# 1/rms rows by a store and a broadcast load instead of TensorE spreads, block differences on VectorE, another order of the first x loads

## The chip, the cores and the metric

The kernel runs on one core of a Trainium2 chip. The metric is the time of one execution in device microseconds (us). Runs of the kernel before took 1004.34, 1004.38 and 1006.59 us, with a median of 1004.38.

## The reference

One layer of a decoder for 2048 prompt tokens and 8 decode tokens, model width 1024, all in float32:

```python
h = rmsnorm(x, norm_g)                    # x * rsqrt(mean(x*x) + eps) * g
p = h @ w_in                              # 1024 -> 8 groups of 512 columns
rq, rk, rv, rg, hq, hf, hi, hgate = split(p, 8)
o_ret = decay_recurrence(rotary(rq), rotary(rk), rv, fixed decay per head)   # 4 heads of 128
o_hg  = decay_recurrence(silu(hq), (1 - lb) * sigmoid(-hf), hi, learned decay)   # 4 heads of 128
o_ret = head_rmsnorm(o_ret, ret_g) * silu(rg);  o_hg = head_rmsnorm(o_hg, hg_g) * silu(hgate)
y = rmsnorm(x + concat(o_ret, o_hg) @ w_out, final_norm_g)
```

It returns y for both kinds of token and the final states. What the change touches is the factor 1/rms = rsqrt(mean(x*x) + eps) of the first rmsnorm, one number for each token.

## The kernel before

**Products.** Each float32 operand is split into a high and a low part, and a product is three matmuls (high by high, high by low, low by high). Most of the large products are products of 2×2 blocks done with seven products of sums and differences of blocks: weights A11, S1, S2, S4, A12, S3, A22 against x blocks B11, T1, T2, B22, B21, T3, T4 (in the value phase the roles are exchanged). One such product for a 512-column tile is twelve matmuls of 128x512, called a position here; seven positions are a unit. PSUM tiles of a unit are called aV, eV, bV in the value phase (aG, aR, aH later).

**Order of the work.** Code puts its steps on a heap by position (`at(pos, f)`, and `after(d, f)` for d positions later); most positions are numbers of the table AT. They are taken off in order of position, and each engine then runs its own instructions in that order: TensorE, VectorE, ScalarE, POOL (GpSimd) and SP, which issues most of the loads. An engine that waits holds up everything queued behind it.

**Phases.** First comes a warm-up of TensorE: 13 matmuls of 128x128 and AT['wu'] tiny ones (L203). Then the value phase makes the columns rv and hi for eight groups of 256 tokens, in the order 4, 5, 6, 7, 0, 1, 2, 3 (V_ORDER; `i` is the place in it, so that group 6 is i=2). The groups i=0 and 1 are done by plain products (L465, PSUM tile pv), those from i=2 on in units of seven positions (L872). Then come 24 units for the other six column groups, the recurrences between them, and eight output units.

**1/rms in the value phase.** For each group, `stats_load` (L324) loads x rows with tokens on the partitions (tiles xn), ScalarE squares and sums them (L332), and POOL makes 1/rms of it (`root`, L336 and L229) into rs_all, tokens on the partitions. But x is multiplied in its transposed form (tiles xr, loaded by `tok_load`, L312, 512 KB for each of two halves), with tokens along the row: there 1/rms must lie along the row and be the same on all partitions. For that `spread_dg` (L356) lets VectorE multiply an identity by 1/rms, twice for a group, and `spread` (L363) multiplies these diagonals by a matrix of ones on TensorE; PSUM tile prs then holds the row on all partitions. `tok_norm` (L372) multiplies x by g and by prs on VectorE. `tok_sums` (L393 to L399) forms the block sums S1 to S4, `s_split` (L271, L272) splits them into s2S, s3S and so on (the number is i).

**The same elsewhere.** For the decode tokens `decode_dg` and `decode_spread` (L583) do this with 8 columns. For the second swap of x blocks, `x1_dg` and `x1_spread` make two rows of 512 tokens by a diagonal, four matmuls (`blk_spread`, L701, PSUM tile prb), a copy on ScalarE and a store by POOL into rb_dram, which `x1_rb` loads eight times (L1345).

**Block differences.** For i=6 and 7, `blocks_sums` (L424 to L439) forms T1 to T4 of x in two halves (n), four subtractions each (tiles bT, bs), and POOL stores them (L430). `less` (L434) puts the halves (6, 0) and (7, 1) on VectorE, (6, 1) and (7, 0) on POOL.

**Buffers.** Short-lived tiles come from a round of buffers (`t_get`, `t_done`): the one that was given back longest ago is used next, so that a tile more or fewer changes which buffer every later tile gets. Weights of a unit are loaded 5.6 positions ahead of it, and first used on VectorE 2.4 positions ahead of it.

The value outputs are added up in tiles vo (L716, from PSUM) and stored into v_dram by SP (L461).

Of the kernel before, what the change touches and what calls it, by code (L numbers as in the profile page):

```python
# [19 lines left out]
P = 128  # L20
# [28 lines left out]
def spooled(u):  # L49
# [79 lines left out]
 'wu': 17,  # L129
# [14 lines left out]
 'dhs': (-5.0, -2.2, -2.2, -1.5)}  # L144
# [5 lines left out]
def step_kernel(ctx, tc, a, out):  # L150
# [22 lines left out]
    vd_dram = dr.tile([2, NB, GW], F32, tag="vd_dram", name="vd_dram")  # L173
    v_dram = [
# [151 lines left out]
    def stats_sum(i, ahead=False):  # L326
        p = V_ORDER[i]
        ms = sm.tile([P, 4], F32, tag="ms", name=f"ms{p}")
        for j in range(2):
            for h in range(2):  # L330
                r = xn.pop((2 * p + j, h))
                act.activation(r, r, AF.Square, accum_out=ms[:, 2 * h + j : 2 * h + j + 1])  # L332
                t_done(r)

        def root():
            pool.tensor_tensor(ms[:, 0:2], ms[:, 0:2], ms[:, 2:4], op=ALU.add)  # L336
            rsqrt_mean(rs_all[:, 2 * p : 2 * p + 2], ms[:, 0:2], D, EPS)

        if ahead:
            root()  # L340
        else:
            after(0.5, root)
# [7 lines left out]
    dgs = {}  # L350

    def spread_dg(i):
        dgs[i] = []
        for c in (2 * V_ORDER[i], 2 * V_ORDER[i] + 1):
            dg = vq.tile([P, P], F32, tag="dg", name=f"dg{c}", bufs=2)
            dve.tensor_scalar(dg, ident, rs_all[:, c : c + 1], None, op0=ALU.mult)  # L356
            dgs[i].append(dg)

    def spread(i):
        p = V_ORDER[i]  # L360
        pt = ps_tr.tile([P, 2, P], F32, tag="tr", name=f"prs{p}")
        for j, dg in enumerate(dgs[i]):
            pe.matmul(pt[:, j], ones, dg, start=True, stop=True)  # L363
        spread_to[i] = pt.rearrange("p a b -> p (a b)")
# [59 lines left out]
    def blocks_sums(i, n):  # L424
# [8 lines left out]
        def less(o, x, y):  # L433
            (dve if (i, n) in ((6, 0), (7, 1)) else pool).tensor_tensor(o, x, y, op=ALU.subtract)  # L434
# [35 lines left out]
    def tok_load0(i, k0, cuts=1):  # L470
        r = x0r[i, k0] = t_get([P, 2, 256], f"x0r{i}{k0}")
        for n in range(0, 2, 2 // cuts):
            kk = slice(n, n + 2 // cuts)
            sp.dma_start(r[:, kk], a["x_t"][V_ORDER[i], :, k0 + kk.start : k0 + kk.stop])
# [101 lines left out]
    dgd = vq.tile([NB, NB], F32, tag="dgd", name="dgd")  # L576

    def decode_dg():
        dve.tensor_scalar(dgd, ident[:NB, :NB], rsd[:, 1:2], None, op0=ALU.mult)

    def decode_spread():
        pt = ps_tr.tile([P, NB], F32, tag="tr", name="prsd")
        pe.matmul(pt, ones[:NB, :], dgd, start=True, stop=True)  # L583
        rb = vq.tile([P, NB], F32, tag="rbd", name="rbd")
        act.activation(rb, pt, AF.Copy)
        dve.tensor_tensor(
            xz[:, : 32 * KT].rearrange("p (k b) -> p k b", b=32)[:, :, :NB], xs,
            rb.unsqueeze(1).to_broadcast([P, KT, NB]), op=ALU.mult,
# [12 lines left out]
    tok_load0(0, 0, 2)  # L601
    wv_load(0, 2)
    act.activation(lb[:, 0:1], zero, AF.Sigmoid)
    tok_load0(0, 4)
    wv_load(4, 2)
    for k in (0, 4):
# [43 lines left out]
    with tc.manual_schedule(engines=ORDERED):  # L650
# [15 lines left out]
        spread_dg(2)  # L666
        ps = plain_next(1, 1, lambda: spread(2))
# [30 lines left out]
    def blk_spread(blk, dg, dst):  # L698
        pt = ps_tr.tile([P, 4, P], F32, tag="tr", name=f"prb{blk}")
        for j in range(4):  # L700
            pe.matmul(pt[:, j], ones, dg[:, j], start=True, stop=True)  # L701
        act.activation(dst, pt.rearrange("p a b -> p (a b)"), AF.Copy)

# [89 lines left out]
    def prep_events(u):  # L793
# [6 lines left out]
        for n, name in enumerate(("A11", "S3", "A22", "A12")):  # L800
            at(U + {0: -7.6, 1: -8.6}.get(u, w["load"] if u % 3 or u >= 12 else w["load0"]) + 0.5 * n, lambda name=name: w_load(u, name))
        if u < 12:
# [6 lines left out]
            at(U + d["sel"], lambda: dec_sel(u))  # L809
        at(U + w["S1"], lambda: w_s1(u))  # L810
# [501 lines left out]
    rb_dram = dr.tile([2, P, GW], F32, tag="rb_dram", name="rb_dram")  # L1312

    def x1_dg(n):
        dg = xd["dg", n] = t_get([P, 4, P], f"dgx{n}")
        dve.tensor_tensor(
            dg, ident.unsqueeze(1).to_broadcast([P, 4, P]),
            rs_all[:, 8 + 4 * TB[n] : 12 + 4 * TB[n]].unsqueeze(2).to_broadcast([P, 4, P]), op=ALU.mult,
        )

    def x1_spread(n):
        dg, rb = xd.pop(("dg", n)), t_get([P, GW], f"rbx{n}")
        blk_spread(2 + n, dg, rb)
        t_done(dg)

        def store():
            pool.dma_start(rb_dram[n], rb)
            t_done(rb)

        after(0.5, store)  # L1330

# [11 lines left out]
    def x1_rb(n, k):  # L1343
        xd["rb"] = t_get([P, GW], f"rb{n}{k}")
        sp.dma_start(xd["rb"], rb_dram[n])  # L1345
# [353 lines left out]
    V_POS = dict(norm=(2.1, 3.1), half=(4.7, 7.6), sums=(4.1, 6.0), s=(5.2, 6.7, 8.6, 9.6), blocks=(5.0, 5.8))  # L1699
    for i in range(2, 7):  # L1700
        U = 7 * (i - 8)
        at(U + 0.3, lambda i=i: spread_dg(i + 1))
        at(U + 1.6, lambda i=i: spread(i + 1))
# [8 lines left out]
        if i < 6:  # L1712
            at(U + 2.7, lambda i=i: tok_load(i + 2))
            at(U + 0.8, lambda i=i: stats_load(i + 2))
            at(U + 3.2, lambda i=i: stats_sum(i + 2))
# [6 lines left out]
    at(-42 + 5.2, decode_norm)  # L1722
# [12 lines left out]
    at(-21 + 3.6, decode_dg)  # L1735
    at(-21 + 5.6, decode_spread)
# [16 lines left out]
    def rec_events(u):  # L1753
# [7 lines left out]
        for n, pos in AT["ret" if u % 3 else "hgrn"].items():  # L1761
# [8 lines left out]
    for n in range(2):  # L1770
        at(9.2 + n, lambda n=n: x1_dg(n))
        at(10.6 + n, lambda n=n: x1_spread(n))
# [144 lines left out]
```

## Time and profile before

| | |
|---|---|
| median of three runs | 1004.38 us |
| the profiled execution | 1006.96 us |
| its span in the trace | 1005.2 us |
| TensorE busy | 987.3 us, 98% |
| VectorE busy | 783.6 us, 78% |
| ScalarE busy | 574.6 us, 57% |
| POOL busy | 256.2 us, 25% |
| DMA | 244.56 MB, mean 243 GB/s |

Times in the views are microseconds from the start of the span. PE is TensorE's matmul side and PEld its weight loads; DVE is VectorE, ACT ScalarE, SPq the queue of SyncE. A row of a timeline has start, duration, engine, line of the kernel, operation, output and inputs, shape and the count of like instructions in a row; `[0.16 <-DVE dg L356]` at its end is idle time of the engine ahead of the row and what released it. Float32 matmuls that aren't split, such as the spreads, are recorded as two passes each. Matmuls overlap, so the time that one takes of TensorE is read from the distance of the starts and not from the duration.

### The profile page before, as it was taken

How to read it: one execution, taken by the hardware profiler on the slowest of the kernel's cores; microseconds unless marked ns; L12 is line 12 of the kernel's file. 1: busy time of each engine (PE TensorE's matmuls, PEld its weight loads, DVE VectorE, ACT ScalarE, POOL GpSimd, SP SyncE). 2: the span in 40 equal slices, each digit the busy share in tenths (PEclk: the TensorE clock that was granted, in tenths of full speed). 3: DMA queues.
4: the chain of work that ended last, by engine and by line, in shares of the span. 5: the costliest groups of instructions: out<-in, count | busy, mean ns of one | idle time of the engine just before them, and what ended most of it. 6: DMA issues, size and time to landing. Idle time of an engine off the chain costs nothing.

```text
span 1005.2 us, 22979 instructions
## 1 busy us (share of the span) xinstructions
PE 987.3 (98%) x8824; PEld 822.0 (82%) x8824; DVE 783.6 (78%) x1361; ACT 574.6 (57%) x1348; POOL 256.2 (25%) x404
## 2 busy tenths in 40 slices
PE   9999999999999999999999999999999999999997
PEld 8788877888888888888788788888888878877885
DVE  6797696879869978887898766877866799767774
ACT  7754523847655664765885555456467577524332
POOL 0211271112332433232012222222222602313121
PEclk9999999999999999999999999999999999999999
DMA  9746659838958878785985993993996396674522
GB/s 332 242 150 238 222 189 357 313 114 298 305 171 306 304 239 287 279 253 184 348 261 175 303 321 119 304 335 109 309 370 218 111 406 228 238 263 155 206 88 83
DMA packets 121340, 244.56 MB, mean 243 GB/s; under 512 B 12128, under 2 KB 52448, under 8 KB 118544
## 3 DMA queue, kind: packets, MB, share of 16 engines
q1 hardware_dynamic: 97968, 164.68, 48.9%
q0 software_dynamic: 22976, 78.17, 21.0%
q8 instruction: 69, 1.13, 0.5%
q14 instruction: 39, 0.32, 0.1%
q10 hardware_dynamic: 288, 0.27, 0.1%
HBM read 155.97 MB, written 90.24 MB: 245 GB/s over the span
## 4 chain that ended last, share of the span: by engine, by line
PE 84%; DVE 7%; ACT 4%; issue 2%; DMA 1%; POOL 1%; POOLq 0%; SPq 0%; DVEq 0%; ACTq 0%
PE aH L872 9%; PE aG L872 8%; PE aO L872 7%; PE aR L872 7%; PE aV L872 5%; PE eG L872 4%; PE eH L872 4%; PE pv L465 4%; PE eO L872 4%; PE eR L872 3%; PE eV L872 2%; PE bH L872 2%; PE bG L872 2%; PE bO L872 2%; PE bR L872 2%
## 5 line engine op out<-in xcount | busy, mean ns | idle before, releaser
L1639 ACT ACTIVATE yj<-xro 128x512 f32<-128x512 f32 x24 | 15.2, 632 | 66.9 <-DVE xro L716 33.2
L1202 ACT ACTIVATE qh<-kh 128x1024 f32<-128x1024 f32 x24 | 25.5, 1061 | 47.3 <-DVE kh L1188 47.3
L1188 DVE TENSOR_TENSOR kh<-kh,fph 128x512 f32<-128x512 f32 x48 | 32.9, 686 | 11.4 <-PE plh L1223 10.5
L949 ACT ACTIVATE sg<-g 128x512 f32<-128x512 f32 x26 | 16.4, 631 | 36.3 <-DVE g L716 35.8
L1082 ACT ACTIVATE obh<-poh 128x128 f32<-128x128 f32 x64 | 16.9, 287 | 32.5 <-PE poh L1078 32.5
L1191 DVE TENSOR_TENSOR qth<-qth,fph 128x512 f32<-128x512 f32 x48 | 32.9, 685 | 0.0
L1082 ACT ACTIVATE obr<-por 128x128 f32<-128x128 f32 x64 | 16.8, 276 | 27.3 <-PE por L1078 27.3
L716 DVE TENSOR_TENSOR xro<-aO,xro 128x512 f32<-128x512 f32 x33 | 22.5, 685 | 8.1 <-PE aO L872 7.8
L1106 POOL DMA_DIRECT2D o_dram<-gth x16 | 12.4, 773 | 62.6 <-DVE gth L1103 23.4
L1090 ACT ACTIVATE obh<-poh,orsh 128x128 f32<-128x128 f32 x64 | 18.2, 366 | 16.5 <-POOL orsh L229 16.4
L336 POOL TENSOR_TENSOR ms<-ms 128x2 f32<-128x2 f32 x8 | 3.0, 370 | 95.4 <-ACT xn L332 95.4
L956 POOL DMA_DIRECT2D g_dram<-g x31 | 16.9, 548 | 39.0 <-DVE g L952 33.9
L1090 ACT ACTIVATE obr<-por,orsr 128x128 f32<-128x128 f32 x64 | 18.2, 368 | 14.6 <-POOL orsr L229 14.6
L228 POOL TENSOR_SCALAR orsh<-omsh 128x4 f32<-128x4 f32 x16 | 4.9, 308 | 84.1 <-ACT obh L1082 83.8
L902 ACT ACTIVATE vo<-aV 128x512 f32<-128x512 f32 x12 | 7.1, 592 | 32.4 <-PE aV L872 32.1
L1069 DVE SCALAR_TENSOR_TENSOR sth<-sth,fph,puh 128x128 f32<-128x128 f32 x48 | 16.7, 347 | 11.0 <-PE poh L1078 8.5
L1106 POOL DMA_DIRECT2D o_dram<-gtr x16 | 12.5, 782 | 46.3 <-DVE g L716 14.0
L1076 PE MATMUL poh<-vh,A 128*128 128x128 f32 x128 | 24.0, 274 | 0.0
L1076 PE MATMUL por<-vr,A 128*128 128x128 f32 x128 | 24.0, 274 | 0.0
L228 POOL TENSOR_SCALAR orsr<-omsr,pk 128x4 f32<-128x4 f32 x16 | 7.6, 474 | 57.5 <-ACT obr L1082 57.5
L1653 DVE SCALAR_TENSOR_TENSOR xro<-xro,yms,fg 128x1024 f32<-128x1024 f32 (+1 forms) x16 | 19.9, 1245 | 3.0 <-POOL yms L1650 3.0
L1078 PE MATMUL poh<-sth,qth 128*128 128x128 f32 x112 | 21.7, 275 | 0.0
(1712 smaller groups left out, 3760.0 us busy)
## 6 DMA issues: line engine op xcount, KB each, us to landing
xn<-in_x_prompt SPq DMA_DIRECT2D x32, 256.0 KB, 4.7
v_dram<-vo SPq DMA_DIRECT2D x32, 256.0 KB, 3.4
xro<-in_x_prompt SPq DMA_DIRECT2D x16, 512.0 KB, 5.8
g_dram<-g POOLq DMA_DIRECT2D x31, 256.0 KB, 5.6
out_y_prompt<-xro POOLq DMA_DIRECT2D x15, 512.0 KB, 3.4
xr<-in_x_t SPq DMA_DIRECT2D x12, 512.0 KB, 5.7
vh<-v_dram SPq DMA_DIRECT2D x16, 256.0 KB, 8.0
gth<-g_dram SPq DMA_DIRECT2D x16, 256.0 KB, 6.8
```

The source lines that it names most:

```text
L465: pe.matmul(ps, xx, ww, start=(first and n == 0), stop=(last and n == 2))
L716: dve.tensor_tensor(o, x, y, op=ALU.add)
L872: pe.matmul(ps, w[i], x[j], start=(first and k == 0 and m == 0), stop=(k == 3 and m == 2), skip_group_check=True,)
L1076: pe.matmul(po[:, j], s_ctx["A"][:, c], box["v"][g][:, j], start=True, stop=src is None)
L1078: pe.matmul(po[:, j], qcol(c), src, start=False, stop=True)
L1082: act.activation(ob[:, j], po[:, j], AF.Square, accum_out=ms[:, j : j + 1])
L1090: act.activation(ob[:, j], po[:, j], AF.Copy, scale=rs[:, j : j + 1])
L1106: after(AT["gate"]["tr"], lambda: pool.dma_start(o_dram[c0 : c0 + 4, ty, :, h].rearrange("c p t -> p c t"), gt.rearrange("p (c t) -> p c t ...
L1188: dve.tensor_tensor(kv[:, :, 0, :], kv[:, :, 0, :], two[:, :, 1:2].to_broadcast([P, nb, b]), op=ALU.mult)
L1191: dve.tensor_tensor(qv[:, :, 1, :], qv[:, :, 1, :], two[:, :, 0:1].to_broadcast([P, nb, b]), op=ALU.mult)
L1202: act.activation(kept_k, k, AF.Copy)
L1653: dve.scalar_tensor_tensor(x[:, cc], x[:, cc], ms[:, 0:1], fg[:, cc], op0=ALU.mult, op1=ALU.mult)
```

## The change

There are four parts.

1. 1/rms goes through DRAM. `root` also stores the 256 numbers of its group into rs_dram (POOL's queue), and `spread` is now a load of them by SP, broadcast to all partitions, into an SBUF tile rsb, which `tok_norm` reads. The diagonals and the matmuls are gone. The decode row goes the same way (store at position −35 + 3.6, load at −35 + 5.6, the multiply stays at −21 + 5.6), and `x1_rb` loads from rs_dram, so that `x1_dg`, `x1_spread`, `blk_spread` and rb_dram are gone.
2. All subtractions of `blocks_sums` are on VectorE.
3. The first x rows and weights are loaded in another order: the first k-slice of x's first half, the first weights, the first slice of the second half, the next weights, and then the two other slices.
4. AT['wu'] is 38 instead of 17.

The diff also names a few positions in the table ('vp', 'vl', 'hd', 'retL', 'hgrnL', 'w24'); they hold the numbers that stood there or in the code before, so these lines are left out here.

```diff
- 'wu': 17,
+ 'wu': 38,
...
+    rs_dram = dr.tile([T // P, P], F32, tag="rs_dram", name="rs_dram")
...
             rsqrt_mean(rs_all[:, 2 * p : 2 * p + 2], ms[:, 0:2], D, EPS)
+            pool.dma_start(rs_dram[2 * p : 2 * p + 2].rearrange("c p -> p c"), rs_all[:, 2 * p : 2 * p + 2])
...
-    def spread_dg(i):
-        dgs[i] = []
-        for c in (2 * V_ORDER[i], 2 * V_ORDER[i] + 1):
-            dg = vq.tile([P, P], F32, tag="dg", name=f"dg{c}", bufs=2)
-            dve.tensor_scalar(dg, ident, rs_all[:, c : c + 1], None, op0=ALU.mult)
-            dgs[i].append(dg)
-
     def spread(i):
         p = V_ORDER[i]
-        pt = ps_tr.tile([P, 2, P], F32, tag="tr", name=f"prs{p}")
-        for j, dg in enumerate(dgs[i]):
-            pe.matmul(pt[:, j], ones, dg, start=True, stop=True)
-        spread_to[i] = pt.rearrange("p a b -> p (a b)")
+        spread_to[i] = vq.tile([P, 2 * P], F32, tag="rsb", name=f"rsb{p}", bufs=2)
+        sp.dma_start(spread_to[i].rearrange("p (c t) -> p c t", c=2), rs_dram[2 * p : 2 * p + 2].partition_broadcast(P))
...
-            (dve if (i, n) in ((6, 0), (7, 1)) else pool).tensor_tensor(o, x, y, op=ALU.subtract)
+            dve.tensor_tensor(o, x, y, op=ALU.subtract)
...
-    tok_load0(0, 0, 2)
+    tok_load0(0, 0, (0,))
     wv_load(0, 2)
     act.activation(lb[:, 0:1], zero, AF.Sigmoid)
-    tok_load0(0, 4)
+    tok_load0(0, 4, (0,))
     wv_load(4, 2)
+    tok_load0(0, 0, (1,))
+    tok_load0(0, 4, (1,))
...
-        spread_dg(2)
-        ps = plain_next(1, 1, lambda: spread(2))
+        spread(2)
+        ps = plain_next(1, 1)
...
     def x1_rb(n, k):
         xd["rb"] = t_get([P, GW], f"rb{n}{k}")
-        sp.dma_start(xd["rb"], rb_dram[n])
+        c = 8 + 4 * TB[n]
+        sp.dma_start(xd["rb"].rearrange("p (c t) -> p c t", c=4), rs_dram[c : c + 4].partition_broadcast(P))
...
-    at(-21 + 3.6, decode_dg)
-    at(-21 + 5.6, decode_spread)
+    at(-35 + 3.6, decode_dg)
+    box_d = {}
+    at(-35 + 5.6, lambda: box_d.update(t=decode_load()))
+    at(-21 + 5.6, lambda: decode_spread(box_d["t"]))
...
-    for n in range(2):
-        at(9.2 + n, lambda n=n: x1_dg(n))
-        at(10.6 + n, lambda n=n: x1_spread(n))
```

What the change moves is shown at three places, in the order in which an engine's instructions stand. On TensorE, in unit i=2 between its second and third product, before (prs7 is the spread for i=3, dg14 and dg15 its diagonals, s2S1 and s2S2 the split sums of i=2):

```order
L872 MATMUL eV341_728<-wvT2l_171,s2S1_629 128x512
L872 MATMUL eV341_728<-wvT2h_170,s2S1_629 128x512
L363 MATMUL prs7_743<-dg14_700,ones_108 128x128
L363 MATMUL prs7_743<-dg15_702,ones_108 128x128
L872 MATMUL aV340_693<-wvB22h_172,s2S2_643 128x512
L872 MATMUL aV340_693<-wvB22l_173,s2S2_643 128x512
```

And at the same place now:

```order
L898 MATMUL eV341_745<-wvT2l_193,s2S1_651 128x512
L898 MATMUL eV341_745<-wvT2h_192,s2S1_651 128x512
L898 MATMUL aV340_714<-wvB22h_194,s2S2_665 128x512
L898 MATMUL aV340_714<-wvB22l_195,s2S2_665 128x512
L898 MATMUL aV340_714<-wvB22h_194,s2S2_665 128x512 x2
```

The two matmuls of the spread are gone, and the products follow each other.

On SP, ahead of unit i=2, before (xn are x rows for the sums of squares, xr70 and xr71 the transposed x of i=3, vo101 and vo111 value outputs that are stored):

```order
L324 DMA xn150_518<-in_x_prompt 128x512
L324 DMA xn151_520<-in_x_prompt 128x512
L312 DMA xr70_534<-in_x_t 128x1024
L312 DMA xr71_535<-in_x_t 128x1024
L461 DMA v_dram11_102<-vo101_538 128x512
L461 DMA v_dram11_102<-vo111_589 128x512
L324 DMA xn00_720<-in_x_prompt 128x512
```

And now, with the broadcast load for i=2, rsb6:

```order
L361 DMA xn150_544<-in_x_prompt 128x512
L361 DMA xn151_546<-in_x_prompt 128x512
L349 DMA xr70_560<-in_x_t 128x1024
L349 DMA xr71_561<-in_x_t 128x1024
L488 DMA v_dram11_103<-vo101_564 128x512
L391 DMA rsb6_576<-rs_dram_99 128x256
L488 DMA v_dram11_103<-vo111_611 128x512
L361 DMA xn00_737<-in_x_prompt 128x512
```

The load stands behind both loads of xr for i=3 and behind the store of vo101, which waits for ScalarE.

On VectorE, in the unit of i=5, before (S3_6 and S4_6 are block sums of i=6, xz the decode input, vo511 and vo522 value outputs of i=5):

```order
L272 TENSOR_TENSOR s6S1_1339<-S1_6_1313,s6S1_1339 128x512
L716 TENSOR_TENSOR vo511_1213<-bV374_1332,vo511_1213 128x512
L586 TENSOR_TENSOR xz_156<-pk_148,rbd_1356 128x8x8
L398 TENSOR_TENSOR S3_6_1365<-xr20_1104 128x512
L399 TENSOR_TENSOR S4_6_1366<-xr21_1105,S2_6_1314 128x512
L716 TENSOR_TENSOR vo522_1238<-aV370_1195,vo522_1238 128x512
```

And now (bT161, bT261 and bs61 are the differences of the second half of i=6):

```order
L309 TENSOR_TENSOR s6S1_1346<-S1_6_1320,s6S1_1346 128x512
L740 TENSOR_TENSOR vo511_1221<-bV374_1339,vo511_1221 128x512
L614 TENSOR_TENSOR xz_178<-pk_170,rbd_1023 128x8x8
L461 TENSOR_TENSOR bT161_1362<-bs61B12_1297,xr20_1115 128x512
L461 TENSOR_TENSOR bT261_1363<-bs61B22_1299,bT161_1362 128x512
L461 TENSOR_TENSOR bs61B12_1297<-bs61B22_1299,bs61B12_1297 128x512
L461 TENSOR_TENSOR bs61B22_1299<-xr21_1116,bT261_1363 128x512
L425 TENSOR_TENSOR S3_6_1368<-xr20_1115 128x512
L426 TENSOR_TENSOR S4_6_1369<-xr21_1116,S2_6_1321 128x512
L740 TENSOR_TENSOR vo522_1246<-aV370_1207,vo522_1246 128x512
```

Four subtractions now stand on VectorE ahead of the sums S3 and S4 of i=6 and of the value output vo522.

## The prediction on record

> **What bounds the kernel now.** I first read the stretches of the span by engine. These are three stretches of 20 us of the value phase and the sum over the span:
>
> ```profile
> core 0: us, PE busy (x) PEld busy (x) DVE busy (x) ACT busy (x) POOL busy (x), PEclk, DMA share, GB/s
> 80.00:100.00 20.00, 20.00 (x92) 16.62 (x91) 15.02 (x29) 9.46 (x20) 2.67 (x5) 1.00 0.62 216
> 120.00:140.00 20.00, 20.00 (x89) 15.91 (x89) 18.59 (x27) 8.44 (x19) 13.13 (x14) 1.00 0.60 207
> 140.00:160.00 20.00, 19.61 (x87) 15.90 (x86) 16.23 (x24) 6.84 (x11) 12.44 (x13) 1.00 0.79 258
> sum 1005.20, PE 987.35 PEld 821.99 DVE 783.60 ACT 574.60 POOL 256.24; mean PE 65.82 PEld 54.80 DVE 52.24 ACT 38.31 POOL 17.08
> ```
>
> TensorE is busy for 987.35 of 1005.20 us at clock 1.00, so 17.85 us of idle are left, and in the value phase it hardly idles at all. A matmul taken out of that phase shortens the span; a wait put into it lengthens it. VectorE is second, and between 120 and 160 us it is nearly full. I then read the chain of waits, which shows the unit of the work: one position, twelve matmuls of 512 columns.
>
> ```profile
> 55.05 2.72 PE aV L872 x12
> ```
>
> So one matmul takes 2.72 / 12 = 0.227 us of TensorE's time, and two take 0.454.
>
> **What the change removes from TensorE.** The rows of the removed matmuls, each call recorded as two passes (median 275 ns, which overlap):
>
> ```profile
> L363 PE MATMUL prs<-dg,ones x24: 272/275/348, 40.7 to 136.9; 128*128 128x128 f32 x24
> L701 PE MATMUL prb<-dgx,ones x8: 272/275/275, 205.7 to 206.5; 128*128 128x128 f32 x8
> L701 PE MATMUL prb<-big,ones x8: 272/275/275, 209.3 to 210.1; 128*128 128x128 f32 x8
> 127.62 0.38 PE L583 MATMUL prsd<-dgd,ones 8*128 8x8 f32 x2
> ```
>
> That is 24 + 16 + 2 = 42 passes. What a pass costs is read from TensorE's timeline, where four stand between two matmuls of unit i=2:
>
> ```profile
> 60.10 0.40 PE L872 MATMUL eV<-wvT2h,s2S 128*128 128x512 f32 x1
> 60.34 0.61 PE L363 MATMUL prs<-dg,ones 128*128 128x128 f32 x4
> 60.70 0.47 PE L872 MATMUL aV<-wvB22h,s2S 128*128 128x512 f32 x1
> 61.01 0.39 PE L872 MATMUL aV<-wvB22l,s2S 128*128 128x512 f32 x1
> ```
>
> From 60.10 to 61.01 are 0.91 us, of which two matmuls of 512 take 0.454: four passes cost 0.456, one 0.114. So 42 × 0.114 = 4.79. The first spread, prs6, costs more, since TensorE waits there for the diagonal:
>
> ```profile
> 40.19 0.39 PE L465 MATMUL pv<-B12h,x0B11l 128*128 128x512 f32 x1
> 40.74 0.68 PE L363 MATMUL prs<-dg,ones 128*128 128x128 f32 x4 [0.16 <-DVE dg L356]
> 41.18 0.47 PE L465 MATMUL pv<-wvT3h,x0B21h 128*128 128x512 f32 x1
> 41.49 0.39 PE L465 MATMUL pv<-wvT3l,x0B21h 128*128 128x512 f32 x1
> ```
>
> From 40.19 to 41.49 are 1.30, less 0.454 is 0.85, that is 0.39 more than the 0.456 counted. Together **−5.18**, all of it on the path, as TensorE has no slack there. What these matmuls had on other engines (twelve diagonals and two large ones on VectorE, three copies on ScalarE, two stores on POOL) goes too, beside TensorE's work, and counts only where VectorE is late (below). The nine added stores on POOL queue behind its own means and square roots; POOL works 256 of 1005 us: nothing. The eight loads of x1 now read what was stored some hundred us earlier; before, one waited for its source:
>
> ```profile
> SPq L740 <- DMA rb_dram<-rbx: 16.9, 1, 16.9
> ```
>
> TensorE has no wait at that place, so its going gives nothing. The decode row is stored and loaded two units ahead of its multiply: nothing. The new table numbers repeat the old ones, and `wu` is all that differs.
>
> **The start.** The warm-up runs 42 more tiny passes. The rows before:
>
> ```profile
> 5.92 0.48 PE L203 MATMUL wu<-ones 128*32 128x8 f32 x34
> 6.33 0.49 PE L465 MATMUL pv<-wvT1h,x0B11h 128*128 128x512 f32 x1
> 6.80 0.50 PE L465 MATMUL pv<-wvT1l,x0B11h 128*128 128x512 f32 x1
> 7.14 0.39 PE L465 MATMUL pv<-wvT1h,x0B11l 128*128 128x512 f32 x1
> ```
>
> 34 passes take 6.33 − 5.92 = 0.41, 12 ns each; 42 more take 0.51, and the first product starts at 6.84. Before, the second one came 0.47 behind the first, not 0.227, because its weights were being split. With the first weights ahead of x's second block in SP's queue they are ready sooner, so this gap closes, and the third stands at 6.84 + 0.454 = 7.30 against 7.14: **+0.16**. The new order of the first x rows can't bring more, as the product stands behind the warm-up. Bounds: 0, if the gap was all that counted, and +0.51, if it stays.
>
> **The first broadcast load, rsb6.** This load (128 partitions × 1 KB) takes the place of the spread for i=2. In SP's queue it stands behind both xr7 loads and one value store:
>
> ```profile
> 39.82 0.93 SPq L312 DMA_DIRECT2D xr<-in_x_t  x2
> 40.85 5.04 SPq L461 DMA_DIRECT2D v_dram<-vo  x2
> ```
> ```profile
> DMA to landing us min/median/max: 4.3/5.7/7.9
> ```
>
> Both xr7 loads (512 KB each) are issued at about 39.8 and 40.3; by the median of such loads the second lands at 46.0. rsb6 is issued at about 41.3. No row shows such a small broadcast load; I take it to land right behind the two, at 46.5, by the nearest row. Now VectorE's timeline, for i=2 and i=3:
>
> ```profile
> 41.91 1.65 DVE L372 SCALAR_TENSOR_TENSOR xr<-xr,g_in,prs 128x256 f32<-128x256 f32 x4
> ...
> 45.80 0.48 DVE L356 TENSOR_SCALAR dg<-ident,rs_all 128x128 f32<-128x128 f32 x2 [2.24 <-POOL rs_all L229]
> ...
> 56.98 0.69 DVE L272 TENSOR_TENSOR s2S<-S,s2S 128x512 fp32r<-128x512 f32 x1
> ...
> 61.88 1.65 DVE L372 SCALAR_TENSOR_TENSOR xr<-xr,g_in,prs 128x256 f32<-128x256 f32 x4
> ...
> 67.72 0.68 DVE L233 TENSOR_TENSOR x0B11l<-xr,x0B11h 128x512 fp32r<-128x512 f32 x1
> ```
>
> The multiplies wait until 46.5 rather than 41.91, 4.6 us. Behind them on VectorE everything of i=2 is queued. The idle 2.24 and the diagonals' 0.48, both gone, take up 2.7; the rest, 1.9, arrives at s2S: it ends at 56.98 + 0.69 + 1.9 = 59.6, where TensorE, now 0.46 earlier, wants it at 60.25. With the longest landing, 7.9, another 2.2 are lost: 61.8, a stall of 1.5. The splits on ScalarE and VectorE wait for each other several times in between, which can lengthen the delay, so I take the middle, **+0.7** out of 0 to 1.5.
>
> Later loads are issued further ahead. rsb7 stands behind the last of the four xn loads:
>
> ```profile
> 59.34 0.33 SPq L324 DMA_DIRECT2D xn<-in_x_prompt  x1
> ```
>
> It is issued at 59.7 and lands between 64.0 and 65.4 (landing 4.3 to 5.7), so the multiply of 61.88 moves by 2.1 to 3.5. x0B11l would then end at 70.5 to 71.9 instead of 68.4, and TensorE takes it here:
>
> ```profile
> 72.14 0.39 PE L872 MATMUL aV<-wvT1h,x0B11l 128*128 128x512 f32 x1
> ```
>
> By the diagonals' 0.48 that are gone there is still room: nothing, with a wait of some tenths as the bad end. The loads of the next three groups stand at the same place in the queue: nothing.
>
> **The subtractions move to VectorE.** Here VectorE takes eight subtractions of POOL, 0.66 each in a row, four for i=6 and four for i=7. The first row is a sum of VectorE during POOL's subtractions, the second POOL's store behind them, the third TensorE waiting for VectorE:
>
> ```profile
> 131.41 2.02 DVE L399 TENSOR_TENSOR S<-xr,S 128x512 f32<-128x512 f32 x1
> ```
> ```profile
> 137.66 1.47 POOL L430 DMA_DIRECT2D x_dram<-bT  x2
> ```
> ```profile
> 151.23 0.47 PE L872 MATMUL aV<-wvT1h,x0B11h 128*128 128x512 f32 x1 [0.39 <-DVE vo L716]
> ```
>
> The sum takes 2.02 where such an operation elsewhere takes 0.69 (56.98): it is stretched while POOL computes. From 80 to 100, where POOL does little, the mean of VectorE's instructions is 15.02 / 29 = 0.52; from 120 to 140 it is 18.59 / 27 = 0.69. Without POOL's subtractions 27 × 0.52 + 4 × 0.66 = 16.7, less than 18.59; likewise 24 × 0.52 + 2.64 = 15.1 from 140 to 160, less than 16.23. So VectorE becomes freer, and TensorE's 0.39 at 151.23 go: **−0.39**, with B below as the other end. The Trainium skill, "GPSIMD Engine Reference", section 8 "Key points", says that GpSimd shares its SBUF interfaces with VectorE and that they contend when VectorE's instruction has two SBUF inputs. The 2.02 agrees. By that rule the multiplies, which now read 1/rms from SBUF instead of PSUM, can be stretched too, but POOL hardly computes while they run: the sum is the same.
>
> **Sum.** −5.18 + 0.16 + 0.7 − 0.39 = −4.71. The profiled execution took 1006.96 (span 1005.2, 1.76 around it), 2.6 above the median of the runs shown, 1004.38. On it the change gives 1002.2; on the median, which I forecast, **999.7**. A measurement tells about 0.3% of this kernel, 3.0 us, from no change: faster is below 1001.4, slower above 1007.4.
>
> **Rivals.** E: rsb6 lands early. If a small load doesn't wait for the large ones ahead of it, the 2.24 idle covers it, and the 0.7 goes: 999.0. For it speaks the smaller size, against it the queue. The Trainium skill, "DMA: Bandwidth & Descriptors", section "Anatomy of one DMA", gives a DMA about 2.0 us plus bytes at 436 GB/s (measured for copies that GpSimd issues); for 128 KB that is an estimate of 2.3 us, landing at 43.6. For xr's 512 KB it gives 3.2, where the trace has 5.7: these loads share the engines with others.
>
> A: broadcast loads late at every group. If the four groups behind i=2 lose 0.7 each as i=2 does, 2.8 more: 1002.5. Against it speaks the room shown at 72.14; for it, that rsb7 may be held by the xn load ahead of it.
>
> B: VectorE becomes the bound at i=6 and i=7, because the stretch isn't POOL's doing. TensorE waits for VectorE already at 151.23, so what is added ahead of that lands on it: 4 × 0.66 − 0.48 = 2.16, and as much for i=7, +4.3 instead of −0.39: 1004.4. Against it stand 2.02 against 0.69.
>
> C, slower: the temporary buffers are handed out round by round, and without the four for the diagonals and their copies every buffer from about 205 us on has another last user. A weight load then can get one that is still to be stored. The longest wait of such a kind is the 16.9 above; loads are issued 3.2 positions ahead of their use, 8.7 us. So 8.2 us would reach TensorE, once: 999.7 + 8.2 = 1007.9. It decides as soon as a wait exceeds 8.7. Against it: the 16.9 cost TensorE nothing, and buffers in a round are mostly long free.
>
> **How the numbers follow.** Forecast 0.57, E 0.20, A 0.11, B 0.05, C 0.07. Below 1001.4 lie the forecast and E, but for the 0.02 of the forecast where rsb6 takes its longest and the start its worst (999.7 + 0.8 + 0.35 = 1000.9, and another late load): faster 0.75. Within 0.3% lie this 0.02, A and B: 0.18; slower is C, 0.07. The range reaches from E, less a twentieth of TensorE's 17.85 idle that other buffers may as well spare it (999.0 − 0.9 = 998.1), less the 0.16 of the start, 997.9, up to A, 1002.5; B and C, 0.12, and some tails are left out.
>
> **What would show it.** No spreads on TensorE and its matmuls in an unbroken row at 41, 60 and 127; the first product at 6.8; VectorE's first multiply of i=2 at about 46.5, waiting for rsb6, and a wait of TensorE for s2S at about 60; between 120 and 160 no VectorE row over 0.7 and TensorE without a wait at 151. I am wrong if TensorE waits over 1 us at any of the starts of i=2 to i=7, if VectorE is fuller than before from 120 to 160, or if behind 205 us a weight load waits for a store and TensorE for it.

## The result and the profile after

The changed kernel takes 1050.07 us (median of five runs, 1048.06 to 1050.65) against 1004.38 before: a ratio of 1.0442, with a 95% interval of 1.0425 to 1.0458. By the ratio it is slower by 44 us, where 4.7 less were forecast. Its span is 1047.7, and the page shows where the time is missing:

```profile
span 1047.7 us, 22975 instructions
PE 989.4 (94%) x8824; PEld 822.4 (78%) x8824; DVE 779.5 (74%) x1354; ACT 573.6 (55%) x1345; POOL 250.8 (24%) x403
```

TensorE has as many matmuls as before (8824, as 42 passes went and 42 came) and is busy as long, but it stands still 40 us longer (1047.7 − 989.4 = 58.3, against 17.85). The stretches of the span by engine (columns as in the prediction) say when. The first row is the kernel before, the others are the changed one:

```profile
40.00:60.00 20.00, 19.84 (x90) 16.23 (x89) 17.59 (x34) 10.46 (x21) 1.07 (x3) 1.00 0.52 181
```
```profile
40.00:60.00 20.00, 14.24 (x63) 11.45 (x61) 4.21 (x7) 4.94 (x12) 3.54 (x6) 0.98 0.96 173
60.00:80.00 20.00, 9.79 (x36) 7.67 (x36) 16.44 (x29) 8.97 (x16) 0.79 (x1) 0.68 0.24 81
80.00:100.00 20.00, 17.95 (x78) 14.57 (x79) 13.62 (x24) 12.32 (x27) 5.11 (x9) 1.00 0.62 137
100.00:120.00 20.00, 9.82 (x44) 7.80 (x42) 7.60 (x16) 5.66 (x15) 3.65 (x6) 0.84 0.75 148
160.00:180.00 20.00, 13.81 (x53) 10.66 (x52) 13.56 (x21) 4.09 (x7) 5.84 (x8) 0.91 0.80 197
```

All of it is lost in the value phase: the product that started at 154.07 before starts at 196.65, 42.6 later, and from there to the end the distance stays between 40 and 43. Two things are seen beside the idle TensorE. From 40 to 60 the DMA engines are 96% busy and move 173 GB/s, where before 52% moved 181. And behind the long waits the granted clock is 0.68 and 0.84, so that TensorE works more slowly, too.

The waits of TensorE (us in total, times, the longest) show the first products of units, aV, waiting for an engine that is itself late. These three rows come to 39.3 us:

```profile
PE aV L898 <- DVE vo L740: 19.8, 4, 12.6
PE aV L898 <- ACT vo L622: 15.7, 1, 15.7
PE aV L898 <- DVE xz L614: 3.8, 1, 3.8
```

Now the timeline of i=2, one row from each engine in the order in which they hang together: POOL's store of 1/rms, SP's broadcast load of it, VectorE's first multiply, and TensorE's first product of the unit with the beginning of the next one:

```profile
42.07 0.78 POOL L375 DMA_DIRECT2D rs_dram<-rs_all  x1 [0.29 <-POOL rs_all L266]
```
```profile
55.09 0.33 SPq L391 DMA_DIRECT2D rsb<-rs_dram  x1
```
```profile
61.37 1.67 DVE L399 SCALAR_TENSOR_TENSOR xr<-xr,g_in,rsb 128x256 f32<-128x256 f32 x4 [17.16 <-DMA rsb<-rs_dram]
```
```profile
69.95 0.80 PE L898 MATMUL aV<-wvT1h,x0B11h 128*128 128x512 f32 x1 [15.70 <-ACT vo L622]
...
74.13 0.39 PE L898 MATMUL eV<-wvT2h,s2S 128*128 128x512 f32 x1
```

The store is issued at 42.07, and SP can issue the load only at 55.09, when the store has landed: 13 us for 1 KB. VectorE goes on 6.3 us after that. VectorE idles for 17.16, TensorE for 15.70, and the first product then takes 74.13 − 69.95 = 4.18 instead of 2.72, at the lower clock. The landing times of both new kinds of transfer (the second line of each is its minimum, median and maximum; of the loads the trace has the landing of two only):

```profile
L375 POOL DMA_DIRECT2D rs_dram<-rs_all x8: 776/790/958, 21.2 to 157.9; - x8
...
DMA to landing us min/median/max: 8.8/10.0/13.0
```
```profile
L391 SPq DMA_DIRECT2D rsb<-rs_dram x6: 326/390/425, 55.1 to 177.0; - x6
...
DMA to landing us min/median/max: 5.1/5.4/5.7
```

So there were three theories at the outset. Theory 1, the chain: a load waits 10 us for its store and lands 5.4 later. Theory 2, congestion: the store itself, 256 separate elements of 4 bytes, fills the DMA engines and makes everything else late. Theory 3, the rival of both, puts the time down to the other parts of the change.

### The profile page after: what moved, and what is told of

It reads as the page before. It is cut to its first block, busy times and chain, and to the rows that moved or that the text cites. A ratio compares the mean times of both kernels' runs of the same rounds, so it can differ in the third digit from the quotient of the medians.

```text
span 1047.7 us, 22975 instructions
## 1 busy us (share of the span) xinstructions
PE 989.4 (94%) x8824; PEld 822.4 (78%) x8824; DVE 779.5 (74%) x1354; ACT 573.6 (55%) x1345; POOL 250.8 (24%) x403
## 3 DMA queue, kind: packets, MB, share of 16 engines
q8 instruction: 69, 1.13, 0.5%
## 4 chain that ended last, share of the span: by engine, by line
PE 65%; issue 9%; DVE 4%; DMA 2%; ACT 2%; POOL 2%; SPq 0%; POOLq 0%; DVEq 0%; ACTq 0%
PE aO L898 7%; PE aH L898 7%; PE aR L898 7%; PE aG L898 7%; PE eG L898 4%; PE eO L898 4%; PE eH L898 4%; PE eR L898 3%; PE bH L898 2%; PE bG L898 2%; PE bO L898 2%; PE bR L898 2%; PE pur L1079 1%; PE puh L1079 1%; PE por L1102 1%
## 5 line engine op out<-in xcount | busy, mean ns | idle before, releaser
L1646 ACT ACTIVATE yj<-xro 128x512 f32<-128x512 f32 x31 | 19.6, 632 | 81.0 <-DVE xro L740 46.7
L898 PE MATMUL aV<-wvT1h,x0B11h 128*128 128x512 f32 x24 | 11.9, 495 | 36.9 <-DVE vo L740 17.4
L399 DVE SCALAR_TENSOR_TENSOR xr<-xr,g_in,rsb 128x256 f32<-128x256 f32 x48 | 20.0, 479 | 33.7 <-DMA rsb<-rs_dram 33.7
L898 PEld LDWEIGHTS aV<-wvT1h,x0B11h 128*128 128x128 f32 x24 | 5.6, 231 | 40.0 <-issue 20.9
L369 ACT ACTIVATE xn<-xn 128x512 f32<-128x512 f32 x32 | 19.8, 623 | 17.5 <-DMA xn<-in_x_prompt 17.5
L1116 ACT ACTIVATE obh<-poh,orsh 128x128 f32<-128x128 f32 x64 | 18.1, 366 | 16.4 <-POOL orsh L266 16.3
L1095 DVE SCALAR_TENSOR_TENSOR sth<-sth,fph,puh 128x128 f32<-128x128 f32 x48 | 16.7, 347 | 9.7 <-PE poh L1104 7.2
L1132 POOL DMA_DIRECT2D o_dram<-gtr x16 | 12.5, 782 | 43.8 <-DVE qth L1217 15.7
L975 ACT ACTIVATE sg<-g 128x512 f32<-128x512 f32 x20 | 12.6, 632 | 18.4 <-DVE g L740 18.1
```

The costliest lines, as they stand in the source:

```text
L399: dve.scalar_tensor_tensor(r[:, k], r[:, k], g_in[:, kk : kk + 1], spread_to[i], op0=ALU.mult, op1=ALU.mult)
L898: pe.matmul(ps, w[i], x[j], start=(first and k == 0 and m == 0), stop=(k == 3 and m == 2), skip_group_check=True,)
L1116: act.activation(ob[:, j], po[:, j], AF.Copy, scale=rs[:, j : j + 1])
L1132: after(AT["gate"]["tr"], lambda: pool.dma_start(o_dram[c0 : c0 + 4, ty, :, h].rearrange("c p t -> p c t"), gt.rearrange("p (c t) -> p c t ...
```

## The experiments

**Stores alone, loads alone, both without a dependence.** The first of three kernels adds to the kernel before nothing but the stores:

```diff
             rsqrt_mean(rs_all[:, 2 * p : 2 * p + 2], ms[:, 0:2], D, EPS)
+            pool.dma_start(rs_dram[2 * p : 2 * p + 2].rearrange("c p -> p c"), rs_all[:, 2 * p : 2 * p + 2])
```

> The kernel before with the eight stores of 1/rms by POOL added (256 elements of 4 bytes each) and nobody reading them. Theory 1 (chain: what costs is that a broadcast load has to wait for its store to land, about 10 us, and then lands 5.4 us later): nothing waits here, so 1004, at most 1007. Theory 2 (congestion: a store of 256 single elements occupies the DMA engines for about 10 us and every other transfer beside it lands late): x and value transfers land late here too, 1015 to 1040. Theory 3 (the other edits cost the time: subtractions on VectorE, order of the first loads, warm-up): 1004.

Measured: 1038.92 against 1006.76 on the same chip, ratio 1.0326 (1.0289 to 1.0363), that is 33 us for eight stores of 1 KB that nobody reads. In its trace the stores land as the first view shows. The second is the stretch right behind the store of 42.06, and the third the same stretch of the kernel before:

```profile
L339 POOL DMA_DIRECT2D rs_dram<-rs_all x8: 772/788/948, 22.3 to 146.2; - x8
...
DMA to landing us min/median/max: 9.0/10.5/13.9
```
```profile
42.50:47.00 4.50, 3.65 (x18) 3.13 (x19) 2.10 (x5) 0.00 (x0) 0.34 (x1) 1.00 0.73 61
```
```profile
42.50:47.00 4.50, 4.50 (x22) 3.71 (x21) 2.26 (x7) 4.08 (x10) 1.07 (x3) 1.00 0.91 315
```

The DMA engines are busy for 73% of that stretch and move 61 GB/s instead of 315. What is under way beside the store lands late: x's transposed rows (xr) in a median of 11.8 us instead of 5.7 over the page, the value stores in 7.9 instead of 3.4. Here no load waits for a store. ScalarE gets the rows for the sums of squares late, so 1/rms is late, so the diagonals of the old spread are late:

```profile
56.14 0.63 ACT L333 ACTIVATE xn<-xn 128x512 f32<-128x512 f32 x1 [13.90 <-DMA xn<-in_x_prompt]
```
```profile
61.78 0.48 DVE L358 TENSOR_SCALAR dg<-ident,rs_all 128x128 f32<-128x128 f32 x2 [10.77 <-POOL rs_all L230]
```

TensorE waits for these diagonals, and at the first product of i=2 for a copy that stands on ScalarE behind the late rows:

```profile
PE prs L365 <- DVE dg L358: 14.5, 3, 10.1
PE aV L874 <- ACT vo L596: 10.2, 1, 10.2
```

The second kernel is the changed one with the loads alone, reading an input. It leaves 1/rms out of the result, as do the third and those with early loads below; the count and the size of the loads stay.

```diff
-            pool.dma_start(rs_dram[2 * p : 2 * p + 2].rearrange("c p -> p c"), rs_all[:, 2 * p : 2 * p + 2])
...
-        sp.dma_start(spread_to[i].rearrange("p (c t) -> p c t", c=2), rs_dram[2 * p : 2 * p + 2].partition_broadcast(P))
+        sp.dma_start(spread_to[i], a["final_norm_g"][256 * (p % 4) : 256 * (p % 4) + 256].partition_broadcast(P))
```

> The changed kernel without the stores of 1/rms; the broadcast loads read the same number of bytes of an input instead (1/rms is left out of the computation, its place is taken by numbers of final_norm_g). Theory 1 and theory 2 both: the loads are early, TensorE does not wait at the first product of i=2, about 1000. Theory 3: about 1045, since all other edits are in. If broadcast loads themselves are slow (5.4 us to land behind others), 1000 to 1010.

Measured: 1018.43, ratio 1.0116 (1.0091 to 1.014). That is neither 1000 nor 1045: the stores explain most, but not all. VectorE's multiply of i=2 waits for the load, which is issued at 42.7. Behind the multiply, ScalarE's copy of a PSUM tile is late, and TensorE waits for it at the first product of i=2:

```profile
50.18 1.67 DVE L398 SCALAR_TENSOR_TENSOR xr<-xr,g_in,rsb 128x256 f32<-128x256 f32 x4 [8.02 <-DMA rsb<-in_final_norm_g]
```
```profile
58.04 0.67 ACT L621 ACTIVATE vo<-pv,rs_all 128x512 f32<-128x512 f32 x1
```
```profile
58.76 0.50 PE L897 MATMUL aV<-wvT1h,x0B11h 128*128 128x512 f32 x1 [4.41 <-ACT vo L621]
```

The third has the same loads and the stores too, so that nothing waits for a store:

> The changed kernel with its stores of 1/rms, but the broadcast loads read an input instead (1/rms is left out of the computation, as in the run without stores), so that no load waits for a store. Theory 1: about 1000, as without the stores. Theory 2: between the run without stores and the changed kernel, 1015 to 1040, the more the nearer to the changed kernel's 1050. Difference to the run without stores = price of congestion; difference to 1050 = price of the chain.

Measured: 1056.36, ratio 1.0503 (1.0478 to 1.0529), no faster than the changed kernel. The load of i=2 waits for no store, and still SP comes to it only at 50.82, since what stands ahead of it in the queue is late itself (the xn loads go on until 47.7, and a value store comes at 49.63):

```profile
50.82 0.33 SPq L391 DMA_DIRECT2D rsb<-in_final_norm_g  x1
```

Theory 1 falls as the cause of the loss: without the dependence nothing is gained. Theory 2 stands. Whether an element holds up the DMA engines themselves or the memory that they write to, no run here shows.

**Elements of 8 bytes, and rows of 512.** In the first, 1/rms of a token pair lies side by side in DRAM, and the multiplies read it in steps of two:

```diff
-            pool.dma_start(rs_dram[2 * p : 2 * p + 2].rearrange("c p -> p c"), rs_all[:, 2 * p : 2 * p + 2])
+            pool.dma_start(rs_dram[p], rs_all[:, 2 * p : 2 * p + 2])
```

> The changed kernel with 1/rms stored as 128 elements of 8 bytes instead of 256 of 4 bytes (the order in DRAM is by token pair; the multiplies read the row in steps of two, x1's as two instructions each). If the landing of a store goes by its number of elements, it falls from 10 to about 5 us, and the loss with it: theory 1 takes 5 us off the chain at each group, theory 2 halves the time in which others are held up; both 1005 to 1030. If landing is a fixed cost, 1048 to 1052.

Measured: 1024.16, ratio 1.0172 (1.0157 to 1.0187). Half as many elements take back 27 of the 44 us (1.0442 − 1.0172). The store's median landing falls from 10.0 to 3.9:

```profile
DMA to landing us min/median/max: 3.2/3.9/8.2
```

In the second, the kernel before gets eight stores of 1 KB with two rows of 512 bytes each (numbers that nobody reads; two of the eight could be issued at the program's start, as they wait for nothing):

```diff
+            pool.dma_start(rs_dram[2 * p : 2 * p + 2], ones[0:2, :])
```

> The kernel before with eight more stores by POOL at the place of the 1/rms stores, of the same 1 KB each, but as two rows of 512 bytes (numbers that nobody reads). If it is the number of single elements that costs (theory 2): landing 2 to 4 us instead of 10, and the time of before, 1004 to 1007, against 1039 with the 4-byte elements. If it is one more store at that place, whatever its shape (POOL held up, the stores' writes): 1015 to 1040.

Measured: 1005.95 against 1006.72, ratio 0.9997 (0.9986 to 1.0008): nothing. Its stores:

```profile
L339 POOL DMA_DIRECT2D rs_dram<-ones x8: 545/621/714, 1.5 to 125.9; - x8
...
DMA to landing us min/median/max: 1.6/3.2/5.3
```

Same bytes, same count of stores, and the page even books as many packets for both (23232 in POOL's queue, 256 more than before): what costs is the single elements within. (These rows also come from 2 partitions instead of 128; the store with 8 bytes comes from 128, and lands early too.)

**Loads issued early.** The changed kernel without stores, all six loads at the start:

```diff
+    for i in range(2, 8):
+        sp.dma_start(rsb[i], a["final_norm_g"][128 * (i - 2) : 128 * (i - 2) + 256].partition_broadcast(P))
```

> The changed kernel without the stores, all six broadcast loads of the value phase issued once at the start (of an input; 1/rms is left out of the computation, as in the run with loads alone, which took 1018). If that run lost its time because each load lands 5.9 us after an issue just ahead of its use, the waits of VectorE for rsb go and so do TensorE's at the first products of the units: 999 to 1003. If the eight subtractions or the order of the other loads cost it, it stays at 1012 to 1020.

Measured: 1005.77, ratio 0.9991 (0.9979 to 1.0003). The 12.6 us of the late loads are gone ((1.0116 − 0.9991) × 1006.7), and so are VectorE's waits for them. The gain of the removed matmuls is seen, too, but it doesn't last: against the kernel before, the same product starts 4.8 us earlier at 210 us, 2.9 at 557, 0.6 at the end.

**Buffers as before.** To test the turn of the buffers (C of the prediction), this kernel is the one with early loads, and it takes and returns four buffers where x1's diagonals and their copies were.

> The run with early loads and no stores (1005.8, 1/rms left out of the computation), with four buffers taken and given back at the places where the kernel before took them for x1's diagonals and their copies, so that each later tile gets the buffer that it has before. In the run without that, 4.8 us were gained up to 210 us and all but 0.7 lost again behind it, 1.4 of it in a wait for a weight load. If the other turn of the buffers is the cause: 1001 to 1003. If the late part gives the gain back whatever the buffers are: 1005 to 1006.

Measured: 1005.35, ratio 0.9989 (0.9976 to 1.0003), the time of the run with early loads. So the turn of the buffers doesn't decide it. It isn't without effect: a wait of TensorE for a weight load, 1.4 us with early loads, is gone, and at 250 us the gain is 5.2 instead of 3.2. Later waits and two stretches of 3.4 us at a granted clock of 0.50 (from 396.9 and 813.3) take it back.

**The small parts, each on the kernel before.** The subtractions on VectorE, and both edits of the start:

> The kernel before with the eight subtractions of POOL moved to VectorE and nothing else. The prediction's step: 0.4 less (the wait at the first product of i=7 goes), 1003.9 against 1004.4. Theory 3 (VectorE becomes the bound at i=6 and i=7): 4.3 more. Theory 2 says nothing on it: 1003 to 1005.

Measured: 1007.06 against 1006.72, ratio 1.0003 (0.9991 to 1.0015). Half of the forecast mechanism is seen: the sum of i=6 isn't stretched any more. The other half isn't: TensorE still waits for VectorE at the first product of i=7, for 0.49 us where it was 0.39:

```profile
134.67 0.69 DVE L399 TENSOR_TENSOR S<-xr,S 128x512 f32<-128x512 f32 x1
```
```profile
151.78 0.47 PE L872 MATMUL aV<-wvT1h,x0B11h 128*128 128x512 f32 x1 [0.49 <-DVE vo L716]
```

> The kernel before with the new order of the first loads and 38 tiny warm-up matmuls, nothing else. The prediction's step: 0.16 more, so no difference that can be told. Theory 3 (the start holds up the groups that follow): several us more. Theory 2: no difference.

Measured: 1015.47, ratio 1.0082 (1.0068 to 1.0095). A surprise; so each alone:

> The kernel before with the new order of the first loads, nothing else. If the two slices that now come behind four weight loads make the groups that follow later: up to 8 us more, with the x splits of the second slice and the loads behind them late in the profile. If the warm-up was the cost: no difference. The prediction: 0 to 0.5 less.

Measured: 1006.29 against 1006.63, ratio 0.9998 (0.9989 to 1.0006).

> The kernel before with 38 instead of 17 tiny warm-up matmuls, nothing else. The two start edits together cost 8.3 us. If the 42 passes at the start, 0.5 us, are what costs (everything behind is shifted against the transfers): up to 8; if the order of the loads does: 1004 to 1006. The prediction: at most 0.5 more.

Measured: 1013.99, ratio 1.0071 (1.0054 to 1.0088). Twenty-one tiny matmuls that take half a microsecond cost 7.2. The trace of that kernel has waits of TensorE that nothing released ("issue"), in other places than before. First those of the kernel before, then those of this one:

```profile
PE plh L1223 <- issue: 2.0, 2, 1.0
PE pah L1223 <- issue: 1.5, 1, 1.5
```
```profile
PE bG L872 <- issue: 2.3, 1, 2.3
PE pah L1223 <- issue: 2.2, 1, 2.2
PE plh L1223 <- issue: 1.5, 2, 1.3
```

They stand mostly in and beside the long runs of small matmuls (plh, pah), hundreds of microseconds behind the start. But they come to 6.0 us against 3.5 before, and these 2.5 are only a part of 7.2. Another part is the clock. Right behind the two longest of these waits, and once more at 823 us, the granted clock is 0.50 for 3.4 us, where the kernel before has 1.00. The first of the three stretches:

```profile
218.90:222.30 3.40, 3.40 (x9) 2.69 (x10) 2.84 (x5) 2.33 (x4) 0.30 (x1) 0.50 0.01 3
```

At half the clock each can cost up to 1.7 us, an estimate, so that waits and clock together are of the size of the loss. Not every long wait brings such a stretch: the run with early loads has one of 3.1 us (at 398) and runs at 1.00 behind it.

What puts the waits where they are? The page lists two queues for instructions; this is the line of the larger one, before:

```profile
q8 instruction: 69, 1.13, 0.5%
```

It says 69 packets and 1.13 MB, 16.4 KB each (with 21 calls more, 70 packets). If they are TensorE's, 17648 records (8824 matmuls and as many weight loads) in 1.13 MB make about 64 bytes each: 256 to a packet. The Trainium skill, "Runtime: NRT & Kernel Launch", section "Instruction fetch mechanics", says just this (blocks of 16 KiB, 256 instructions), and that crossing a block is mostly hidden. The first agrees with the packets; the second holds here for all but three of the 69, by the waits without a releaser that are longer than 0.5 us.

The traces confirm it in another way. Number all the records of TensorE's queue in order of their starts, from 0: matmuls, weight loads and, in the kernel before, 189 semaphore and drain instructions. In the 18 traces of this case 52 waits of matmuls without a releaser are longer than 0.5 us, and each one stands ahead of a record whose number leaves 193 or 194 when divided by 256.

A call of the warm-up is four records, so 64 calls are one packet. That is the test:

```diff
- 'wu': 17,
+ 'wu': 81,
```

> The kernel before with 81 tiny warm-up matmuls, 64 more than its 17. Theory of code position: a packet of TensorE's instructions holds 256 (the page: 69 packets, 1.13 MB), and a call of these matmuls is four of them; with 64 calls more, all later instructions lie one whole packet further and at the same place in it, so the waits without a releaser stand where they stood before and only the start is longer, by 128 passes of 12 ns, 1.5 us: 1006 to 1009. Rival (more work at the start shifts everything against the transfers): more than the 7.4 of 21 more calls, 1014 to 1025.

Measured: 1007.63, ratio 1.001 (1.0 to 1.0019), for 64 calls more, where 21 more cost 7.2 us. Two of the three waits stand where they stood before (at 299 and 402 us; 297 and 400 before), and the third, of 1.0, is gone:

```profile
PE pah L1223 <- issue: 1.5, 1, 1.5
PE plh L1223 <- issue: 1.5, 1, 1.5
```

> The kernel before with 49 tiny warm-up matmuls, half a packet of instructions more. Theory of code position: waits without a releaser at other places, of another sum than before's 3.6 us; the time differs from before by more than the 0.8 us that the start is longer, in either direction (998 to 1014). Rival (work at the start): between those of 38 and of 81, 1014 to 1020.

Measured: 1014.22, ratio 1.0073 (1.0059 to 1.0086). So 32 more calls cost 7.3 us, and 64 more 1.0: it is the place in the packet, not the work at the start.

**Parts of the change taken together.** The way through DRAM alone, and the whole change but for the subtractions:

> The changed kernel with its start, warm-up and subtractions put back as before: the way of 1/rms through DRAM alone. If the parts add up: 1050 less 8.3 and 0.3, 1041. If the late groups hide the late start: 1047 to 1050. The stores alone cost 33, and the loads some 5 to 10 beside what the removed matmuls give.

Measured: 1067.43, ratio 1.06 (1.0581 to 1.0619), more than any expectation. 42 passes fewer, without the 42 more at the start, move the later instructions in their packets, and the waits show it:

```profile
PE plh L1247 <- issue: 9.6, 4, 4.5
PE eR L896 <- issue: 1.7, 1, 1.7
PE bR L896 <- issue: 0.9, 1, 0.9
PE pah L1247 <- issue: 0.5, 1, 0.5
```

These are 12.7 us against 3.5 before.

> The changed kernel with four halves of the subtractions back on POOL as before, all else as changed. The way through DRAM alone took 1067, 17 more than the whole change. If the subtractions on VectorE spare that in a kernel whose POOL also issues the stores: 1055 to 1060, with the rest (code position) for the warm-up. If all of the 17 is code position: 1050.

Measured: 1060.22, ratio 1.053 (1.051 to 1.055). So in this kernel, late as it is, the subtractions on VectorE spare some 9 us (1.053 against 1.0442), though they spare nothing where the transfers are on time. Of these, 5.6 are there at the second product of i=7, which starts at 202.22 here and at 196.65 in the changed kernel. The rest of the distance to 1067, 7 us, goes with the start: the waits without a releaser are 3.7 us here and 12.7 there.

**A version for use.** Only x1's rows go through DRAM, made as rows by one matmul and stored in eight elements of 512 bytes; seven more warm-up calls keep the place in the packet.

```diff
+            pe.matmul(pt[:8], rs_all[:, 8:16], ident, start=True, stop=True)
+            act.activation(row, pt[:8], AF.Copy)
+            after(0.4, lambda: pool.dma_start(rs_dram[8:16], row))
```

> A version for use: the kernel before, with only the second swap's rows taken through DRAM, made as rows by one matmul of the eight columns of 1/rms with the identity and stored as eight elements of 512 bytes; the number of TensorE's instructions ahead of the late stages is kept with seven more tiny warm-up matmuls. Theory 2 (elements) and the code position: no delay by the store, 1.81 us of matmuls less, 0.23 and 0.17 more: 1003 to 1004.5 against 1004.4, faster by 0.1%. If stores or broadcast loads cost as such: 1005 to 1010.

Measured: 1008.03 against 1006.29, ratio 1.0007 (0.9994 to 1.0019): no gain. The store lands in 1.6 us and delays nothing, and the product at 210 us starts 1.2 earlier; by 842 it is 1.2 later. What the version had gained it loses from 811 us on, at a wait of 0.9 for ScalarE and at half the clock:

```profile
813.00:820.00 7.00, 6.14 (x44) 4.91 (x45) 6.82 (x12) 6.39 (x15) 0.00 (x0) 0.52 1.01 414
```

The kernel before runs at 1.00 there. No version here is faster than the kernel before beyond the noise.

## Why the prediction was wrong

**The step that failed** is the sentence on the nine added stores: "POOL works 256 of 1005 us: nothing". It counted POOL's time to issue them, 0.8 us each, and asked neither when they land nor what they take from others. Each took 8.8 to 13.0 us to land and kept the DMA engines busy with little moved: 33 us, shown by the run with the stores alone. The prediction's rows were of DMAs of 256 and 512 KB, and the store of 1 KB was given no landing at all. It also let rsb6 be issued at 41.3 without waiting for the store that it reads; but that wait is not what costs, as the run without it is no faster. The store's elements should have been counted: the diff's "c p -> p c" makes 256 of 4 bytes. The Trainium skill says so in "DMA: Bandwidth & Descriptors", section "Rules for kernel authors": a last dimension that isn't contiguous becomes one descriptor per element; and section "Specifications" has line rate from 512 bytes on. The runs agree on the elements: 10.0 us in the median for 256 of 4 bytes, 3.9 for 128 of 8, 3.2 for two of 512. Where between 8 and 512 bytes the limit lies, no run here shows.

**rsb6 and the later loads.** That a small broadcast load lands like the large ones, in about 5.7, was nearly right (5.6 and 6.3 for the two of the six whose landing the run with the loads alone shows). Its price of 0.7 was too small: in the run with loads alone TensorE waits 4.4 us at the first product of i=2, and 1.1 to 1.6 at four of the later units, where nothing was forecast. Altogether it was 12.6. Two steps fell. The load was taken to be issued at 41.3 and there at 46.5; in that run it was issued at 42.7, and VectorE began at 50.18, 7.4 us behind the issue. And the stall was looked for at s2S, at 60; it came at the unit's first product, which waits for ScalarE to copy the PSUM tile of i=1. That copy (58.04) stands on ScalarE behind the splits of x0B11 and x0B21, which wait for the multiplies. The prediction named what is queued behind the multiply on VectorE, and not what is queued behind that on ScalarE. The sign of rival A was right, its 2.8 was too small.

**The removed matmuls**: 5.18 was nearly right for the value phase and x1 (4.8 at 210 us, in the run with early loads). That it would reach the end was wrong. What takes it back isn't the turn of the buffers (C) alone: as they were before, a wait of 1.4 us goes and the end is the same. In the run with early loads the unreleased waits and one wait for a weight load come to 6.9 us against 3.5 before, which is most of it; the rest stays open. So does the reason for which the clock fell at 813 us in the version for use.

**The start.** The +0.16 took `wu` for work at the start, and as that it was small enough: the third matmul starts at 7.18 instead of 7.14. Its other effect was left out: it moves the place of all later instructions in their packets. Here it makes up for the 42 passes that are gone, and without the new start the change was dearer still (1067 against 1060, both with the subtractions as before). Alone it costs 7.2.

**The subtractions**: the stretch of the sum was POOL's, as forecast, but TensorE's wait of 0.39 didn't go (0.49 with the subtractions alone), and VectorE became less free than the means had said: 17.96 and 16.75 us from 120 to 160, where 16.7 and 15.1 were worked out, and 18.59 and 16.23 stood before. The time can't tell (0.9991 to 1.0015).

**The sum.** Early loads −0.9, lateness of the loads +12.6, stores +32.8: 44.5, and the change took 44.4 (0.0442 × 1004.4). That the parts add up so well is in part luck, since loads and stores without a dependence took 50.6 together.

## What to carry to other kernels

Count the elements of a DMA, not its bytes, and what it does to the transfers beside it: eight stores of 1 KB, each of 256 single floats, cost 33 us, and no wait for the stores shows that. A value on the partitions that has to lie along a row can be turned on TensorE, for 0.114 us a pass here, or stored from a tile in which it is a row already, which delayed nothing. And where the bound engine's number of instructions changes, compare the waits that nothing released, and the granted clock, before and after: they may move by more than the instructions were worth.

## What the runs showed beyond that

The place of TensorE's instructions in their packets of 256 is worth some 7 us here (1.0071 and 1.0073 for 21 and 32 calls more), and the old time all but comes back after 64 calls (1.001). All 52 of the longer waits without a releaser stand at one place of the 256. And a TensorE that stood still for 15.7 us started slowly: behind a first interval of 0.59 us (from 69.95) come five of 0.42 to 0.43 rather than 0.227, with a granted clock of 0.50 between 60 and 70 us. Two of these matmuls:

```profile
70.97 0.63 PE L898 MATMUL aV<-wvT1h,x0B11l 128*128 128x512 f32 x1
71.39 0.63 PE L898 MATMUL aV<-wvT1h,x0B11h 128*128 128x512 f32 x1
```

The Trainium skill, "TensorE: Matmul & The Clock Gate", section "Part 1: The HAM clock gate (the "warmup" mystery)", gives 426.7 ns for 512 columns with the array cold; the five intervals agree.
